# The way out of a convolution branch by seven products of quarters, with its weights' sums and the mixing's sums made by transfers in DRAM

## The chip, the cores and the metric

The kernel runs on one core of one Trainium2 chip. A core has five engines with an instruction queue each: TensorE (PE, matrix products; PEld is its weight load), VectorE (DVE), ScalarE (ACT), GpSimd (POOL) and SyncE (SP, which starts most transfers). Sixteen DMA engines move data between DRAM and the on-chip buffers, or from DRAM to DRAM. The metric is the device time of one execution in microseconds.

## The reference

One block of a decoder over 512 tokens of width 1024, all in float32. The part that matters here lies between two token mixers and the residual:

```python
z_glu, z_rx, z_rg, z_ga, z_gb = jnp.split(h @ w_in[l] + b_in[l], split_idx, axis=-1)

u = z_glu[..., :D_CONV] * jax.nn.sigmoid(z_glu[..., D_CONV:])
u = causal_depthwise_conv(u, conv_dw_w[l], conv_dw_b[l])
u = jax.nn.silu(layernorm(u, conv_ln_g[l], conv_ln_b[l]))
y_a = u @ conv_w_out[l] + conv_b_out[l]                    # 512x1024 by 1024x1024
...
y_b = (hb * jax.nn.gelu(z_rg, approximate=True)) @ lru_w_out[l]   # 512x1280 by 1280x1024

m = jax.nn.sigmoid(z_ga) * y_a + jax.nn.sigmoid(z_gb) * y_b
x = x + m @ w_mix_out[l]                                   # 512x1024 by 1024x1024

h = rmsnorm(x, norm2_g[l])
x = x + (jax.nn.silu(h @ ffn_w1[l]) * (h @ ffn_w3[l])) @ ffn_w2[l]
```

## The kernel before

**Products.** Every float32 operand is split into a high part (a cast to fp32r on ACT, `split_to`, L127) and a low part (full minus high, by `sub`, L123, on DVE or POOL), and a product is three matmuls: high by high, high by low, low by high. Channels lie along the 128 partitions and the 512 tokens along the columns, until the mixing turns to tokens by partition.

**Stages.** z is the way in, with the depthwise convolutions, the gates and the recurrence run beside it; yb the recurrence's way out (8 tiles of 128 channels); ya the convolution branch's way out (8 tiles); mxr the mixing's product; fr (L1443) and or the channel mixer. The layer norm of the convolution branch (`conv_norm`) runs beside z and yb: lnms is the all-reduce over partitions of the column sums, lnvs that of the squares, both on POOL; after lnvs ACT takes the root (lnvp) and DVE its RECIPROCAL, and then the eight tiles u are scaled, passed through Silu and split into un.

**ya.** Tile j takes one 1024x128 chunk of `conv_w_out` (co, `w_tiles`), 24 matmuls of 512 columns into one PSUM bank (`mm3`), then on DVE one operation that adds the bias and multiplies by the gate sga, and two adds of 256 columns with yb into mxu and mxv, the mixing's inputs. `mixq.order()` sets the order of the tiles to 0, 4, 1, 5, ..., so that pairs for the mixing come early.

**The mixing and the channel mixer** already use seven products. `Quartered` describes a weight matrix in quarters b11, b12, b21, b22 and its sums t1 = b12 + b11, t3 = b22 + b12, t2 = t3 + b11, t4 = t2 + b21. `Sevenfold` makes the sums of the inputs (`pair`) and runs the seven products in two halves (`run`): the first opens banks r1, r2 and r5, and adds the first two into the residual x (the operations x<-mxr on DVE); the second half opens r1 again and reuses the other banks. For the mixing, `make_sums` loads rows of w_mix_out (mxws) and makes the sums on DVE, four adds for each of four row pairs: t1 and t4 stay on chip and are split there, t2 and t3 are stored to DRAM (mxt) and loaded later as chunks. For the channel mixer's second matrix, `dram_sums` makes the sums (ot) in DRAM by eight transfers for each slice, started by POOL: a copy t <- b (L487), an adding transfer t <- t + b (L488); a step that needs an earlier one waits for its landing.

**Weights** come in chunks in a fixed order (`wchunk`): SP loads a chunk into one of 8 raw buffers (raw), ACT casts it into one of 5 hl buffers, DVE or POOL takes the low part; `weights` emits chunks AHEAD = 4 beyond the one in use. LO_BY_DVE = 6 says that the chunks lo0 to lo5 of yb are split by DVE, lo6 and lo7 by POOL.

**Order.** On PE, ACT, DVE and SP the instructions run in the order of the program, in which work beside a stage is dealt out by generators (`run_beside`); on POOL a scheduler sets the order ahead of time. Each engine works through its queue in order: what waits holds up all behind it.

Of the kernel before, what the change touches and what calls it, by code (L numbers as in the profile page):

```python
# [13 lines left out]
P = 128  # L14
# [43 lines left out]
SUMS_OWN = 40  # L58
LO_BY_DVE = 6


MIX_LATE_LAG, LATE_LAG = 2, 8

# [22 lines left out]
def tile_block(ctx, tc, a, out):  # L86
# [38 lines left out]
    def split_to(h, l, full, eng, copy=act.copy):  # L125

        copy(h, full)  # L127
# [145 lines left out]
    IN_PLACE = ("t2", "t1", "t4", "t3")  # L273

    class Quartered:
        def __init__(self, name, w, kh, lo, parts=(), step=None, on_pool=(), put_off=()):
# [11 lines left out]
            def quarter(n, k):  # L288
                if n[0] == "t":
                    assert self is mixq or out_made  # L290
# [40 lines left out]

        def make_sums(self, k):
            q = [raws.tile([P, 1024], F32, tag="raw", name=f"{self.name}ws{k}_{i}") for i in range(2)]
            for i, v in enumerate(q):
                nc.sync.dma_start(v, self.w[:, self.tile(k, i), :])
            (q11, q12), (q21, q22) = ((v[:, :T], v[:, T:]) for v in q)
            add(q22, q22, q12)
            add(q12, q12, q11)
            add(q11, q22, q11)
            add(q21, q21, q11)  # L340
            for n, v in (("t1", q12), ("t2", q11), ("t3", q22), ("t4", q21)):
                if n in self.parts:
                    self.parts[n][k] = split(f"{self.name}{n}{k}", v, vec)
                else:
                    nc.sync.dma_start(self.sums[n, k], v)
# [137 lines left out]
    def dram_sums(quarter, sums):  # L483
# [5 lines left out]
        return [(copy, t1, b11), (plus, t1, b12), (copy, t3, b12), (plus, t3, b22), (copy, t2, t3), (plus, t2, b11), (copy, t4, t2), (plus, t4, b21)]  # L489

    def out_sums():

        rows = outq.w.rearrange("p (k i) n -> p i k n", i=2)
        jobs = []
        for k0 in range(0, KF, OUT_SUMS_OF):
            ks = slice(k0, min(k0 + OUT_SUMS_OF, KF))
            jobs.append(dram_sums(lambda i, h: rows[:, i, ks, h * T : (h + 1) * T], {n: v[:, ks, :] for n, v in outq.all_sums.items()}))
# [3 lines left out]
        out_made.append(True)  # L501

    for k in BEGUN:
        for n in ("b11", "b21"):
            f_both(n, k, pool_e if (n, k) == ("b11", 2) else None if k == BEGUN[0] else vec)

# [351 lines left out]

    u, un, lanes, held_back = [], [], [], []
    ended, total = [], []  # L860
# [27 lines left out]
    def column_sums(name, tot):  # L888
# [3 lines left out]
        return sums  # L892

    def conv_norm():
        mean = bank2("lnmp")
        sums = column_sums("lnms", total[0])
        yield True
        for _ in range(MEAN_LAG):
            yield True
        act.activation(mean, sums, AF.Copy, scale=1.0 / DC)  # L900
        yield True
        tot = longt("lnvt")
        for c in range(8):
            sub(vec, u[c], u[c], mean)
            q = tot if c == 0 else shortt(f"sq{c}")
            act.activation(q, u[c], AF.Square)
            yield True
            if c:
                vec.tensor_tensor(out=tot, in0=tot, in1=q, op=ALU.add)
# [7 lines left out]
        vec.reciprocal(rs, rs)  # L917
        for _ in range(6):
            yield True
        for c in range(8):  # L920
# [3 lines left out]
            un.append(split(f"un{c}", u[c], vec))  # L924
            yield True

    lanes += [conv_lane(0), conv_lane(1)]
# [192 lines left out]

    sgb, sga = [None] * 8, [None] * 8

    def sig(base, j, ps, dest, name):
        dest[j] = longt(f"{name}{j}")
        act.activation(dest[j], ps, AF.Sigmoid, bias=b_in(base + j))
        yield 0

    def half_sig(j, ps):
        sgb[j] = longt(f"sgb{j}")
        act.activation(sgb[j], ps, AF.Tanh, scale=0.5, bias=b_in(GB + j))  # L1130
        yield 0
# [20 lines left out]
    f_sums_steps = make_f_sums()  # L1152
    out_made = []
    out_steps = out_sums()
    with tc.manual_schedule(engines={ET.PE, ET.Activation, ET.DVE, ET.SP}):
        for kind, j in ORDER:
            next(f_sums_steps, None)
            if kind == "u" and j < EARLY:
                for _ in glu(j, in_mm(GLU + j), in_mm(GLU + 8 + j)):
# [14 lines left out]
            elif kind == "ga":  # L1174
                later(sig(GA, j, step(GA, j), sga, "sga"), 1)
            elif kind == "h":
# [17 lines left out]
    yb = sgb  # L1194
    run_beside(1000)


    LO, HI = HALVES

    class Sevenfold:
        def __init__(self, q, lag=0, behind=False):
            self.lag, self.kept, self.behind = lag, 0, behind
            self.q, self.uv, self.ops, self.waiting = q, [], [], []  # L1210
            self.name, self.kh = q.name, q.kh
# [17 lines left out]
        def pair(self, k, ua, va):  # L1229
# [10 lines left out]
            add(e[:, LO], ua[:, HI], va[:, LO])  # L1240
            self.ops.append((u_, sp, e, va))

# [7 lines left out]
        def run(self, sums, begun, end):  # L1250
# [10 lines left out]
            def split_late():  # L1261
                k = len(late)
                if k < kh:
                    late.append((split(f"{n}eb{k}", self.ops[k][2], vec), split(f"{n}vb{k}", self.ops[k][3], vec)))

            r1, r2 = ([bank(f"{n}{r}{i}") for i in range(2)] for r in ("r1", "r2"))
# [25 lines left out]
            def third(i, ks, closing=kh - 1, cs=slice(0, T), banks=None, opening=None):  # L1292
                for k in ks:
                    self.product(banks or r1, i, quarter(late[k][1], HI), *get(k, "t4"), k == opening, k == closing, not banks, cs)

            for k in range(kh - 1):
                second(k, *get(k, "b22", "t2", "t3"))
                split_late()
# [7 lines left out]
            act.activation(warm, late[-1][1][0][:, :1].bitcast(F32), AF.Sqrt, scale=0.0, bias=eps_t)  # L1306
            last = get(kh - 1, "b22", "t2", "t3", ahead=AHEAD - 1)
            end(lambda: second(kh - 1, *last), plus, less, r1, r2, r7, third)

    m7 = Sevenfold(mixq, MIX_LATE_LAG, True)  # L1310
    for n, j in enumerate(mixq.order()):
        ws = w_tiles(f"co{j}", ND)
        ps = bank(f"ya{j}")
        mm3(ps, ws, un)
        o = sga[j]
        vec.scalar_tensor_tensor(out=o, in0=ps, scalar=pc("conv_b_out", j), in1=o, op0=ALU.add, op1=ALU.mult)
        m7.tile(j, lambda cs, dst: add(dst, o[:, cs], yb[j][:, cs]))
        if n == 0:
            mixq.make_sums(3)
        if n == 5:  # L1320
            x2 = [[longt(f"x2{t}{h}") for h in range(2)] for t in range(NT)]
            for t in range(NT):
                for h in range(2):
                    nc.sync.dma_start(x2[t][h], x_nat[:, t, h * T : (h + 1) * T])
        next(f_sums_steps, None)

# [65 lines left out]

    m7.run(x2, lambda k: None, mix_end)


# [342 lines left out]
```

## Time and profile before

| | |
|---|---|
| time, median of 3 runs | 786.16 us (785.57 to 787.25) |
| the profiled execution | 785.74 us, span 784.0 us |
| granted TensorE clock | 0.999 |
| busy: PE, DVE, ACT, POOL | 99%, 85%, 60%, 33% of the span |
| DMA | 158.65 MB, 202 GB/s in the mean |

The profile is of one execution. Busy times don't add up to the span, since engines run side by side. In lists of instructions, the first number is the start in microseconds from the span's beginning, the second the duration; a group xN is N instructions in a row. Names are written out <- in, and L is the line of the kernel.

### The profile page before, as it was taken

To read this page: it belongs to the slowest core of one execution; us is meant where nothing else is said; L and a number is where in the kernel's file an instruction comes from. 1 tells how busy PE (TensorE), PEld (TensorE's weight loads), DVE (VectorE), ACT (ScalarE), POOL (GpSimd) and SP (SyncE) were. 2 spreads that over 40 slices of the span, in tenths; PEclk is the share of its full clock that TensorE was granted. 3 is DMA by queue.
4 is the path that set the end of the run, shared out by engine and by line. 5 is a ranking of instruction groups with operands and counts; after the bars stand their busy time and mean duration, and the time that the engine had idled before them with its cause. 6 is when DMAs were issued, how large, how long until landed. Compare 5 with 4: busy or idle time off the path is not lost.

```text
span 784.0 us, 12205 instructions
## 1 busy us (share of the span) xinstructions
PE 776.4 (99%) x4325; PEld 679.2 (87%) x4325; DVE 667.9 (85%) x1007; ACT 473.8 (60%) x696; POOL 262.5 (33%) x209
## 2 busy tenths in 40 slices
PE   8999999999999999999999999999999999999997
PEld 8988888888888888888888898999999999888886
DVE  6489998899887996999767869779888889999957
ACT  8543678976785687575234676555554555666844
POOL 3366856577555753130000461312212220000001
PEclk9999999999999999999999999999999999999999
DMA  8827978796783555378565466997989794679522
GB/s 246 233 58 212 250 216 229 201 247 188 210 247 120 165 156 164 120 241 251 199 198 160 153 229 216 233 307 192 270 240 246 250 213 126 230 236 297 171 67 108
DMA packets 181199, 158.65 MB, mean 202 GB/s; under 512 B 14202, under 2 KB 146450, under 8 KB 181138
## 3 DMA queue, kind: packets, MB, share of 16 engines
q1 hardware_dynamic: 171186, 132.43, 57.7%
q0 software_dynamic: 9792, 25.17, 13.1%
q8 instruction: 34, 0.56, 0.3%
q10 hardware_dynamic: 160, 0.27, 0.1%
q14 instruction: 27, 0.22, 0.1%
HBM read 132.14 MB, written 35.65 MB: 214 GB/s over the span
## 4 chain that ended last, share of the span: by engine, by line
PE 98%; DMA 1%; DVE 0%; ACT 0%; SPq 0%; issue 0%
PE z L622 36%; PE fr L1443 25%; PE or L1248 13%; PE yb L622 7%; PE ya L622 6%; PE mxr L1248 5%; PE f L622 3%; PE g L1074 2%; PE fr L1506 1%; DMA x<-in_x_dram 1%; PE tx L683 0%; PE th L667 0%; PE z L740 0%; ACT of L1680 0%; PE orl L1248 0%; DVE n1j L704 0%
## 5 line engine op out<-in xcount | busy, mean ns | idle before, releaser
L875 DVE SCALAR_TENSOR_TENSOR cv<-u,par,cv 128x507 f32<-128x507 f32 (+15 forms) x240 | 162.1, 732 | 4.0 <-ACT cv L871 3.3
L123 POOL TENSOR_TENSOR hl_in<-raw_in,hl_in 128x1024 fp32r<-128x1024 f32 (+1 forms) x52 | 122.8, 2373 | 87.4 <-ACT hl_in L127 83.3
L1443 PE MATMUL fr<-hs_0h,hl_ft 128*128 128x256 f32 x320 | 59.2, 283 | 0.0
L127 ACT CAST hl_in<-raw_in 128x1024 fp32r<-128x1024 f32 x50 | 51.4, 1047 | 1.6 <-PE z L622 0.8
L1443 PEld LDWEIGHTS fr<-hs_0h,hl_ft 128*128 128x128 f32 x320 | 50.6, 192 | 0.0
L1443 PE MATMUL fr<-hs_0l,hl_ft 128*128 128x256 f32 x160 | 45.3, 283 | 0.0
L127 ACT CAST hl_fb<-raw_fb 128x1024 fp32r<-128x1024 f32 x30 | 31.3, 1046 | 23.1 <-PE fr L1443 10.9
L488 POOL DMA_DIRECT2D ot<-in_ffn_w_dram x24 | 26.4, 1112 | 54.2 <-DVE hl_ft L123 32.7
L123 DVE TENSOR_TENSOR hl_fb<-raw_fb,hl_fb 128x1024 fp32r<-128x1024 f32 x29 | 35.3, 1221 | 10.4 <-ACT hl_fb L127 10.4
L123 POOL TENSOR_TENSOR hl_ot<-raw_ot,hl_ot 128x1024 fp32r<-128x1024 f32 x1 | 2.4, 2410 | 121.3 <-ACT hl_ot L127 121.3
L622 PE MATMUL z<-h10h,hl_in 128*128 128x512 f32 (+1 forms) x108 | 41.1, 382 | 0.0
L622 PE MATMUL z<-h12h,hl_in 128*128 128x512 f32 (+1 forms) x108 | 40.8, 379 | 0.0
L622 PE MATMUL z<-h13h,hl_in 128*128 128x512 f32 (+1 forms) x108 | 40.8, 379 | 0.0
L622 PE MATMUL z<-h14h,hl_in 128*128 128x512 f32 (+1 forms) x108 | 40.8, 379 | 0.0
L622 PE MATMUL z<-h15h,hl_in 128*128 128x512 f32 (+1 forms) x108 | 40.8, 379 | 0.0
L622 PE MATMUL z<-h16h,hl_in 128*128 128x512 f32 (+1 forms) x108 | 40.8, 379 | 0.0
L622 PE MATMUL z<-h11h,hl_in 128*128 128x512 f32 (+1 forms) x108 | 40.8, 379 | 0.0
L622 PE MATMUL z<-h17h,hl_in 128*128 128x512 f32 (+1 forms) x108 | 40.8, 379 | 0.0
L127 ACT CAST hl_ft<-raw_fb 128x1024 fp32r<-128x1024 f32 x28 | 28.6, 1048 | 15.0 <-DVE raw_fb L114 11.8
L127 ACT CAST hl_ob<-raw_ob 128x1024 fp32r<-128x1024 f32 (+1 forms) x23 | 23.3, 1015 | 21.1 <-PE or L1248 14.7
L115 POOL TENSOR_TENSOR fws<-fws 128x256 f32<-128x256 f32 x44 | 34.1, 774 | 2.4
L123 DVE TENSOR_TENSOR hl_ft<-raw_fb,hl_ft 128x1024 fp32r<-128x1024 f32 x28 | 33.6, 1218 | 1.2 <-ACT hl_ft L127 1.2
(948 smaller groups left out, 2589.9 us busy)
## 6 DMA issues: line engine op xcount, KB each, us to landing
raw_in<-in_w_in_dram SPq DMA_DIRECT2D x51, 512.0 KB
raw_fb<-in_ffn_w_dram SPq DMA_DIRECT2D x74, 256.0 KB
ot<-in_ffn_w_dram POOLq DMA_DIRECT2D x30, 512.0 KB, 8.6
raw_ob<-in_ffn_w_dram SPq DMA_DIRECT2D x33, 256.0 KB
raw_ot<-ot SPq DMA_DIRECT2D x33, 256.0 KB
fws<-in_ffn_w_dram SPq DMA_DIRECT2D x12, 512.0 KB
raw_lo<-in_lru_w_out_dram SPq DMA_DIRECT2D x16, 320.0 KB
ot<-ot POOLq DMA_DIRECT2D x10, 512.0 KB, 6.2
```

Of the source, the lines that this page charges most:

```text
L115: plus_on = lambda eng, o, x, y: eng.tensor_tensor(out=o, in0=x, in1=y, op=ALU.add)
L123: return eng.tensor_tensor(out=o, in0=x, in1=y, op=ALU.subtract)
L127: copy(h, full)
L488: plus = lambda o, x: pool_e.dma_start(o, x, accum_op=ALU.add)
L622: pe.matmul(ps, l, r, start=i == 0, stop=i == n - 1)
L875: vec.scalar_tensor_tensor(out=acc[:, s:], in0=u[c][:, : T - s], scalar=dw(c, s), in1=acc[:, s:], op0=ALU.mult, op1=ALU.add)
L1074: pe.matmul(ps[:HB], head_chunk[0][:ROWS_G, g, h % 2, m, :], ext[h][m][:ROWS_G], start=m == 0, stop=m == 1)
L1248: pe.matmul(banks[i][:, cs], l_[:, ts], r_[:, cs], start=start and n == 0, stop=stop and n == 2, skip_group_check=again)
L1443: pe.matmul(ps[:, HALVES[i]], lw[:, c, :], rx_, start=not (again or i or c or m), stop=bool(i and c == 3 and m == 2), skip_group_check=True,)
L1506: pe.matmul(self.r4[:, HALVES[i]], lw, rx_, start=not (i or c or m), stop=bool(i and c == 3 and m == 2), skip_group_check=True)
```

## The change

1. The convolution branch's way out is made of quarters. For two groups g of output columns (`CO_PAIRS`), seven products of 128-channel blocks with 256 tokens each: r1 = a11·b11, r2 = a12·b21, r3 = s4·b22, r1 += s2·t2, r5 = s1·t1, r7 = s3·t3, r1 += a22·t4. The inputs' sums s1 to s4 are made on DVE (`ya_sums`) and split (`ya_sum_parts`); gates and results are kept by halves of the tokens (`by_tokens`), so that yb's tiles become the mixing's inputs in place. The weights come as 14 chunks (cob11, cob21, cob22, cot2, cot1, cot3, cot4 for two groups) instead of 8.
2. The sums of the weights of this product and of the mixing are made by `dram_sums`, 16 transfers of 512 KB each (`mid_sums`), started by POOL; `make_sums` goes. The mixing's t1 and t4 are loaded as chunks too.
3. LO_BY_DVE becomes 8, MIX_LATE_LAG 1, the mixing fetches its chunks one less ahead in places, and some splits of the channel mixer's first chunks change between DVE and POOL.

The core of the diff:

```diff
-LO_BY_DVE = 6
+LO_BY_DVE = 8
+MID_AT, MID_STEP = 60, 4
-MIX_LATE_LAG, LATE_LAG = 2, 8
+MIX_LATE_LAG, LATE_LAG = 1, 8
...
-    for j in [0, 4, 1, 5, 2, 6, 3, 7]:
-        wchunk(f"co{j}", conv_out[:, :, j * P : (j + 1) * P], ND, P, lo=vec)
+    CO_PAIRS = ((0, 1), (3, 2))
+    co_sums = {n: dram.tile([P, 2, 4, 2 * P], F32, tag=f"co{n}", name=f"co{n}") for n in IN_PLACE}
...
+    CO_ORDER = [(n, g) for of in (("b11", "b21"), ("b22", "t2", "t1", "t3", "t4")) for g in range(2) for n in of]
...
-    mixq = Quartered("mx", a["w_mix_out"][0].rearrange("(k p) n -> p k n", p=P), ND // 2, vec, ("t1", "t4"), put_off=("b22_2",))
+    mixq = Quartered("mx", a["w_mix_out"][0].rearrange("(k p) n -> p k n", p=P), ND // 2, vec, step=2, on_pool=("t4_0",), put_off=("b22_2",))
...
+    def mid_sums():
+        co_jobs = [dram_sums(lambda i, h: co_quarter(f"b{i + 1}{h + 1}", g), {n: v[:, g] for n, v in co_sums.items()}) for g in range(2)]
+        for name, of in (("co", co_jobs), ("mx", sums_jobs(mixq, 2))):
+            for start, dst, src in (one for step in zip(*of) for one in step):
+                with tc.issue_after(newest["sub"]):
+                    start(dst, src)
+                yield
+            sums_made.append(name)
...
+    def ya_sums(k):
+
+        a1, a2 = u[k], u[k + 4]
+        sub(vec, a2[:, HI], a1[:, HI], a2[:, HI])
+        sub(vec, a1[:, HI], a1[:, LO], a1[:, HI])
+        sub(vec, a1[:, LO], a2[:, HI], a1[:, LO])
+        add(a2[:, LO], a2[:, LO], a1[:, LO])
...
+            if n >= MID_AT:
+                next(mid_steps, None)
...
-        vec.scalar_tensor_tensor(out=sgb[j], in0=sgb[j], scalar=1.0, in1=ps, op0=ALU.add, op1=ALU.mult)
+        for o, cs in by_tokens(j, sgb, "sgb"):
+            vec.scalar_tensor_tensor(out=o, in0=o, scalar=1.0, in1=ps[:, cs], op0=ALU.add, op1=ALU.mult)
         run_beside(7)
         next(f_sums_steps, None)
-        if j in (2, 4, 6):
-            mixq.make_sums(j // 2 - 1)
+        for _ in range(MID_STEP):
+            next(mid_steps, None)
...
-    for n, j in enumerate(mixq.order()):
-        ws = w_tiles(f"co{j}", ND)
-        ps = bank(f"ya{j}")
-        mm3(ps, ws, un)
-        o = sga[j]
-        vec.scalar_tensor_tensor(out=o, in0=ps, scalar=pc("conv_b_out", j), in1=o, op0=ALU.add, op1=ALU.mult)
-        m7.tile(j, lambda cs, dst: add(dst, o[:, cs], yb[j][:, cs]))
...
+    def ya_group(g):
+        k1, k2 = CO_PAIRS[g]
+
+        def product(ps, x_, w_, again=False):
+            h, l = weights(f"co{w_}_{g}")
+            for i in range(2):
+                cols = slice(i * P, i * P + P)
+                for c, (xh, xl) in enumerate(ya_in[x_]):
+                    for m, (lw, rx_) in enumerate(((h, xh), (h, xl), (l, xh))):
+                        pe.matmul(
+                            ps[:, HALVES[i]], lw[:, c, cols], rx_, start=not (again or i or c or m),
+                            stop=bool(i and c == 3 and m == 2), skip_group_check=True,
+                        )
+            return ps
...
+        r1 = product(bank(f"ya1_{g}"), "a11", "b11")
+        c11 = biased("c11", r1, k1)
+        r2 = product(bank(f"ya2_{g}"), "a12", "b21")
+        add(c11, r2, c11)
+        mixed(c11, k1, 0)
+        yield
+        r3 = product(bank(f"ya3_{g}"), "s4", "b22")
+        product(r1, "s2", "t2", True)
+        q = biased("q", r1, k2, -1.0)
+        r5 = product(bank2(f"ya5_{g}"), "s1", "t1")
+        add(q, r5, q)
+        c12 = shortt(f"c12_{g}")
+        add(c12, r3, q)
+        mixed(c12, k2, 0)
+        r7 = product(bank(f"ya7_{g}"), "s3", "t3")
+        sub(vec, q, q, r7)
+        mixed(q, k2, 1)
+        made(k2)
+        c21 = biased("c21", r7, k1)
+        product(r1, "a22", "t4", True)
+        add(c21, r1, c21)
+        mixed(c21, k1, 1)
+        made(k1)
+        yield
```

`biased` is an Identity on ACT with scale and bias, two of 256 columns; `mixed` multiplies by the gate and adds yb's half, on DVE; `made` hands a pair to the mixing.

How the change orders two engines, in rows of the program (name, shape, and a count where rows are alike). On POOL, around the two all-reduces, before (fs is a sum for the channel mixer, hl_lo a low part of yb's weights):

```order
L443 DMA fs3_82<-fws3_1_1_3031 128x4x256
L891 ISA
L891 ISA lnms_3024<-lnmt_1069 128x512
L891 ISA lnvs_3268<-lnvt_3148 128x512
L123 ISA
L123 TENSOR_TENSOR hl_lo6_0_3335<-raw_lo6_0_3333,hl_lo6_0_3335 128x640
L123 TENSOR_TENSOR hl_lo6_1_3340<-raw_lo6_1_3338,hl_lo6_1_3340 128x640
```

And in the changed kernel (L493 is the copying and L494 the adding transfer of `dram_sums`, L911 the all-reduce):

```order
L911 ISA lnms_3044<-lnmt_1077 128x512
L494 DMA cot1_79<-in_conv_w_out_dram 128x4x256 x2
L493 DMA cot3_81<-in_conv_w_out_dram 128x4x256 x2
L493 DMA mxt1_83<-in_w_mix_out_dram 128x2x512
L494 DMA cot3_81<-in_conv_w_out_dram 128x4x256 x2
L493 DMA mxt1_83<-in_w_mix_out_dram 128x2x512
L493 DMA cot2_78<-cot3_81 128x1024 x2
L494 DMA mxt1_83<-in_w_mix_out_dram 128x2x512
L494 DMA cot2_78<-in_conv_w_out_dram 128x4x256
L911 ISA lnvs_3301<-lnvt_3171 128x512
L494 DMA cot2_78<-in_conv_w_out_dram 128x4x256
L493 DMA cot4_80<-cot2_78 128x1024
```

Twelve transfers have come between lnms and lnvs, and the four splits of lo6 and lo7 have left the queue. On DVE, in ya, what stands around a tile before:

```order
L1316 SCALAR_TENSOR_TENSOR sga4_2972<-ya4_3643,par_95,sga4_2972 128x512
L114 TENSOR_TENSOR mxu0_3616<-sga4_2972,sgb4_2065 128x256
L114 TENSOR_TENSOR mxv0_3617<-sga4_2972,sgb4_2065 128x256
L123 TENSOR_TENSOR hl_co3_3686<-raw_co3_3684,hl_co3_3686 128x1024
L123 TENSOR_TENSOR mxus0l_3672<-mxu0_3616,mxus0h_3671 128x512
L123 TENSOR_TENSOR mxs10_3675<-mxv0_3617 128x256
L123 TENSOR_TENSOR mxe0_3680<-mxu0_3616,mxv0_3617 128x256
L123 TENSOR_TENSOR mxs1p0_3677<-mxs10_3675,mxs1p0_3677 128x256
L123 TENSOR_TENSOR mxv0_3617<-mxs10_3675,mxu0_3616 128x256
L114 TENSOR_TENSOR mxe0_3680<-mxu0_3616,mxv0_3617 128x256
L1316 SCALAR_TENSOR_TENSOR sga1_2684<-ya1_3689,par_95,sga1_2684 128x512
```

And around the seventh and eighth products (r5 and r7 of the first group) of the changed kernel:

```order
L124 TENSOR_TENSOR hl_cot2_1_3834<-raw_cot2_1_3832,hl_cot2_1_3834 128x1024
L115 TENSOR_TENSOR q_0_3828<-ya5_0_3831,q_0_3828 128x512
L115 TENSOR_TENSOR c12_0_3862<-ya3_0_3769,q_0_3828 128x512
L124 TENSOR_TENSOR hl_cot1_1_3869<-raw_cot1_1_3867,hl_cot1_1_3869 128x1024
L1394 TENSOR_TENSOR c12_0_3862<-c12_0_3862,sga1_0_2796 128x512
L124 TENSOR_TENSOR q_0_3828<-q_0_3828,ya7_0_3866 128x512
L115 TENSOR_TENSOR sgb1_0_1371<-c12_0_3862,sgb1_0_1371 128x512
L1394 TENSOR_TENSOR q_0_3828<-q_0_3828,sga1_1_2797 128x512
L124 TENSOR_TENSOR hl_cot3_1_3917<-raw_cot3_1_3915,hl_cot3_1_3917 128x1024
L115 TENSOR_TENSOR sgb1_1_1372<-q_0_3828,sgb1_1_1372 128x512
L124 TENSOR_TENSOR mxus1l_3900<-sgb1_0_1371,mxus1h_3899 128x512
L124 TENSOR_TENSOR mxs11_3903<-sgb1_1_1372 128x256
```

In place of one operation on the product and two adds for each tile, DVE has one operation out of PSUM, two on halves of tokens, and a split of a chunk, for each product, with the pairs for the mixing between them.

More of the change, by code (lines that the diff above doesn't have):

```diff
@@ L125, in split_to @@
     def split_to(h, l, full, eng, copy=act.copy):
-        copy(h, full)
+        newest["cast"] = copy(h, full)
         if eng is None:
@@ L919, in conv_norm @@
             yield True
-        for c in range(8):
+        for c in [0, 4, 1, 5, 2, 6, 3, 7]:
             vec.tensor_tensor(out=u[c], in0=u[c], in1=rs, op=ALU.mult)
@@ L1293, in third @@
                 for k in ks:
-                    self.product(banks or r1, i, quarter(late[k][1], HI), *get(k, "t4"), k == opening, k == closing, not banks, cs)
+                    self.product(banks or r1, i, quarter(late[k][1], HI), *get(k, "t4", ahead=self.ahead), k == opening, k == closing, not banks, cs)
             for k in range(kh - 1):
-                second(k, *get(k, "b22", "t2", "t3"))
+                with tc.issue_after(newest["late"]) if self.behind and k == kh - 2 else nullcontext():
+                    got = get(k, "b22", "t2", "t3", ahead=self.ahead if k == kh - 2 else AHEAD)
+                second(k, *got)
                 split_late()
@@ L1306, in run @@
             act.activation(warm, late[-1][1][0][:, :1].bitcast(F32), AF.Sqrt, scale=0.0, bias=eps_t)
[L1307 removed]
+            with tc.issue_after(newest["late"]) if self.behind else nullcontext():
+                last = get(kh - 1, "b22", "t2", "t3", ahead=AHEAD - 1)
             end(lambda: second(kh - 1, *last), plus, less, r1, r2, r7, third)
[L1310 to L1325 removed]
+    m7 = Sevenfold(mixq, MIX_LATE_LAG, True, AHEAD - 1)
@@ L1327, in tile_block @@
+    groups = [ya_group(g) for g in range(2)]
+    for g in groups:
+        next(g)
+    ya_sum_parts()
+    next(groups[0])
+    x2 = [[longt(f"x2{t}{h}") for h in range(2)] for t in range(NT)]
+    for t in range(NT):
+        for h in range(2):
+            nc.sync.dma_start(x2[t][h], x_nat[:, t, h * T : (h + 1) * T])
+    next(groups[1])
     for _ in f_sums_steps:
@@ L1393, in tile_block @@
     m7.run(x2, lambda k: None, mix_end)
+    assert not put_off
     o7 = Sevenfold(outq, LATE_LAG)
```

120 lines of the change are left out of this document (82 added, 38 removed).

## The prediction

> **What bounds the kernel now.** I began with the page's busy times and the chain that ended last, then read the chain in order of time.
>
> ```profile
> span 784.0 us, 12205 instructions
> PE 776.4 (99%) x4325; PEld 679.2 (87%) x4325; DVE 667.9 (85%) x1007; ACT 473.8 (60%) x696; POOL 262.5 (33%) x209
> ...
> PE 98%; DMA 1%; DVE 0%; ACT 0%; SPq 0%; issue 0%
> ```
> ```profile
> 310.61 54.40 PE yb L622 x240
> 365.01 43.52 PE ya L622 x192
> 408.53 35.36 PE mxr L1248 x156
> ...
> 497.81 175.68 PE fr L1443 x1464
> ```
>
> TensorE is the bound: 98% of the chain is its own work. From yb through ya to mxr each piece starts where the last one ended, so in the stages of the change every microsecond of PE is a microsecond of the kernel, and every new wait of PE as well. The profiled execution took 785.74 us, 1.74 more than its span, and 0.42 less than the median of 786.16; I sum against 785.74 and add the 0.42 at the end.
>
> **The products (TensorE).** Before, ya is 192 matmuls of 512 columns: 43.52/192 = 226.7 ns each. Afterwards it is 2 groups x 7 products x 24 = 336 matmuls of 256 columns. Before has that width in the channel mixer: 175.68/1464 = 120.0 ns each. That is more than half of 226.7 (113.3), and this row shows why.
>
> ```profile
> core 0: us, PE busy (x) PEld busy (x) DVE busy (x) ACT busy (x) POOL busy (x), PEclk, DMA share, GB/s
> ...
> 575.00:600.00 25.00, 25.00 (x210) 25.00 (x210) 22.11 (x26) 14.22 (x19) 7.32 (x8) 1.00 0.98 213
> ```
>
> In those 25 us weight loading (PEld) is never idle: 210 loads, 119 ns each, set the pace. So ya becomes 336 x 0.1200 = 40.32 us, and the gain is 43.52 - 40.32 = **3.20 us**, not the eighth (5.44) that the count of products promises. The ends are 0.1133 (38.1 us, gain 5.4) and 0.1200; I take 0.1200, since the new matmuls also have a weight load each. [...]
>
> **The sums' transfers (GpSimd's queue).** 32 transfers of 512 KB, each copying or adding in DRAM, are put between lnms and the end of the branch. GpSimd works in order, and lnvs, the all-reduce of the variance, now stands behind 14 of them, 12 of which come after lnms. What it waits for is a chain: copy t3, add to t3 (waits for that copy), copy t2 from t3 (waits for that add), and the issue of the add to t2, which waits for that copy.
>
> ```profile
> 304.92 3.75 POOL L891 PARTITION_ALL_REDUCE lnms<-lnmt  x1 [5.70 <-DVE y9l L123]
> 325.72 3.65 POOL L891 PARTITION_ALL_REDUCE lnvs<-lnvt  x1 [17.05 <-DVE lnvt L909]
> ```
> ```profile
> L488 POOL DMA_DIRECT2D ot<-in_ffn_w_dram x24: 843/1135/1467, 492.5 to 640.9; - x24
> ...
> DMA to landing us min/median/max: 6.0/9.0/12.0
> ```
> ```profile
> L487 POOL DMA_DIRECT2D ot<-ot x12: 515/522/559, 560.3 to 620.7; - x12
> ...
> DMA to landing us min/median/max: 3.3/6.4/7.4
> ```
> ```profile
> q1 hardware_dynamic: 171186, 132.43, 57.7%
> q0 software_dynamic: 9792, 25.17, 13.1%
> ```
> ```profile
> 300.00:315.00 15.00, 15.00 (x68) 12.40 (x67) 9.05 (x13) 10.57 (x16) 3.75 (x1) 1.00 0.58 185
> 315.00:330.00 15.00, 15.00 (x68) 12.43 (x67) 14.72 (x21) 7.50 (x12) 3.65 (x1) 1.00 0.42 121
> ```
>
> L488 is an adding transfer, L487 a copying one. lnms ends at 308.67; two adds are issued (2 x 0.84), so the copy of t3 goes out at 310.4. With medians: 310.4 + 6.4 + 9.0 + 6.4 + 1.14 (issue) = 333.3, and lnvs ends 3.65 later, at **T = 337.0**, against 329.37 before. The ends: shortest landings give 310.4 + 3.3 + 6.0 + 3.3 + 0.84 = 323.8, earlier than lnvt is ready (325.72), so T stays 329.4; longest give 310.4 + 7.4 + 12.0 + 7.4 + 1.47 + 3.65 = 342.3. I take the medians, which come from stretches with the DMA engines 98% busy, because these will be as busy: q0's 13.1% of 784 us is 103 us for some 48 such transfers, 2.1 us of all sixteen engines each; 14 of them before lnvs are 29 us in some 39, on top of the 0.42 to 0.58 there. [...]
>
> **What waits behind lnvs, on DVE.**
>
> ```profile
> 330.29 3.36 DVE L917 RECIPROCAL lnvp<-lnvp 128x512 f32<-128x512 f32 x1
> 333.56 0.81 DVE L123 TENSOR_TENSOR hl_lo<-raw_lo,hl_lo 128x640 fp32r<-128x640 f32 x1
> ```
> ```profile
> 390.01 0.42 DVE L123 TENSOR_TENSOR mxs<-mxv 128x256 f32<-128x256 f32 x1
> 390.35 0.42 DVE L123 TENSOR_TENSOR mxe<-mxu,mxv 128x256 f32<-128x256 f32 x1
> ...
> 391.25 0.42 DVE L123 TENSOR_TENSOR mxv<-mxs,mxu 128x256 f32<-128x256 f32 x1
> 391.70 0.42 DVE L114 TENSOR_TENSOR mxe<-mxu,mxv 128x256 f32<-128x256 f32 x1
> ...
> 421.49 2.73 DVE L114 TENSOR_TENSOR x<-mxr,x 128x512 f32<-128x512 f32 x4 [3.77 <-PE mxr L1248]
> 424.14 0.68 DVE L123 TENSOR_TENSOR mxeb1l<-mxe,mxeb1h 128x512 fp32r<-128x512 f32 x1
> 424.74 1.22 DVE L123 TENSOR_TENSOR hl_mxt<-raw_mxt,hl_mxt 128x1024 fp32r<-128x1024 f32 x1
> 425.88 0.68 DVE L123 TENSOR_TENSOR mxvb1l<-mxv,mxvb1h 128x512 fp32r<-128x512 f32 x1
> ```
> ```profile
> L1316 DVE SCALAR_TENSOR_TENSOR sga<-ya,par,sga 128x512 f32<-128x512 f32 x8 | 6.0, 750 | 9.9 <-PE ya L622 9.5
> ```
>
> Start to start, DVE's operations cost 0.34 us (256 columns), 0.45 where one needs its forerunner (391.25 to 391.70), 0.60 (512), 0.66 (512 out of PSUM, 2.65/4), 1.14 (1024), 3.27 (the reciprocal); 0.74 for 640 is taken between 0.60 and 1.14. Counted in the new order, from the reciprocal to the first add of the mixer's product into x stand 1 reciprocal, 12 + 40 of 256, 6 of 640, 43 + 10 of 512 and 23 of 1024: 3.3 + 17.7 + 4.4 + 25.8 + 6.6 + 26.2 = 84.0. Before it was 1, 36, 3, 57 and 15, or 69.1 (all 512 at 0.60), and the idle time in ya (9.9) and ahead of the add (3.77) was its cover. Sixteen adds for the mixer's sums go (9.6), but splits of 14 chunks in place of 8, sums of the inputs, mixing by token halves and four splits that GpSimd did (LO_BY_DVE) come.
>
> PE wants that add done when it opens r1's bank again in the mixer's second half.
>
> ```profile
> 426.05 0.62 PE L1248 MATMUL mxr<-hl_mxt,mxvb0h 128*128 128x512 f32 x2
> ...
> 427.41 0.62 PE L1248 MATMUL mxr<-hl_mxb,mxeb0h 128*128 128x512 f32 x2
> ```
>
> Without new waits that moment is 426.05 - 3.20 = 422.85. The add ends at T + 0.92 (329.37 to 330.29) + 84.0 + 0.68 + some 1.5 for operations on a forerunner's result = T + 87.1. The second add follows 1.26 later while PE wants it 0.68 later, another 0.58. So PE stalls S = T + 87.1 - 422.85 + 0.58 = T - 335.2, which is 1.8 at T = 337.0.
>
> There is a **floor that T doesn't move**. DVE can't split cot2_1 before its cast, and ACT does that after q, which needs the sixth product: 365.01 + 6 x 24 x 0.120 = 382.3, then two activations of 0.41 and a cast of 1.05.
>
> ```profile
> 386.85 1.05 ACT L127 CAST hl_mxb<-raw_mxb 128x1024 fp32r<-128x1024 f32 x1 [4.39 <-PE ya L622]
> ...
> 390.46 0.41 ACT L127 CAST mxs1p<-mxs 128x256 fp32r<-128x256 f32 x1 [1.79 <-DVE mxs L123]
> ```
>
> So at 384.2 DVE begins 13 of 1024, 20 of 256, 19 of 512 and 8 out of PSUM: 38.3 us, the add itself 0.68, some 0.7 for forerunners: 423.9, or a stall of 1.0 + 0.58 = **1.6**. The floor's ends are 0 (DVE waits nowhere and PE's demand is read too early) and 3 (each wait for a cast or product costs another 0.1 to 0.2). I take S = 1.6 to 1.8, so 1.7. Afterwards nothing gives it back: PE has no idle time to shrink.
>
> **What else moves, and lies beside.** SP's queue meets the residual's x loads earlier, ahead of half of mxt2_1, whose place in the raw buffers waits for DVE's split of mxb21_0 (near 399 by the prices above), so they go out at about the same time as before, and are needed at that same add, 20 us later.
>
> ```profile
> 401.38 4.07 SPq L1324 DMA_DIRECT2D x<-in_x_dram  x8
> ```
>
> The loads of weights: minus 8 of 512 KB and 8 stores of 256, plus 8 of 256 and 6 of 512, about even at q1's 0.577 x 784/132.43 = 3.4 us per MB. The transfers' 68 us nearly fill the engines from 298 to 400. Followed link by link from T with 6.4 a copy and 9.0 an add, the branch's last sum (t4) lands near 361 and the mixer's near 400; the loads that wait for them on SP, with the channel mixer's first weights behind, get their raw buffers only some 10 us after that. GpSimd's freed time (four splits) and the two new splits for the channel mixer fall where it is idle. If that cover fails, PE waits for a weight, rival 3.
>
> **The sum.** 785.74 - 3.20 + 1.7 = 784.2, and 0.4 more against the median: **784.6**, 1.6 us or 0.2% below; 0.2% (1.57 us) is also about what a measurement of this kernel can tell from no change.
>
> **Rivals.**
> 1. The queue is no matter: transfers land in 3.3 and 6.0 us, T stays below 336, and the floor is at its low end, 0 to 1. For it: 0.42 DMA share at 315 to 330, and 3.77 us of slack ahead of the add. Against: 69 us of DVE's work became 84. Time 783.0 to 783.9.
> 2. The other side: lnvs behind the queue decides. Back-to-back adds and copies queue behind each other, and T passes 340.0, where S = 4.8 and the kernel is 0.2% slower; that takes three landings of 24.8 us together instead of 21.8. The longest rows give T = 342.3, S = 7.1, 790.0. For it: six adds and six copies are issued within some 25 us, and landings of 12.0 are seen. Against: the stretch was half empty.
> 3. The DMA engines are over-full and a chunk of weights or a sum comes late. 68 us of transfers on 0.42 to 0.80 busy stretches leave no room between 300 and 409. If each of some 12 links down to the mixer's t4 takes 1.5 us more, it lands 18 us late, past that 10, and holds back SP's queue and the first weights of the channel mixer: 3 to 8 us, 786 to 791. Against: in 575 to 600 the engines are 98% busy and PE is idle nowhere.
> 4. The narrow matmul costs 0.113: 5.4 instead of 3.2 gained; but PE then comes to the same add 2.2 earlier and waits there, 784.8 by T, or 783.6 where the floor alone rules (its sixth product ends 1.0 earlier, so the stall grows by 1.2).
>
> **Chances.** Forecast (S 1 to 4) 0.45, of which 0.22 faster and 0.23 same. Rival 1: 0.18, faster. Rival 2: 0.20, slower. Rival 3: 0.12, 0.05 same and 0.07 slower. Rival 4: 0.05, 0.02 faster and 0.03 same. Together faster 0.42, same 0.31, slower 0.27. The range leaves out the low tail below 782.8 and rival 2 above 788.6.
>
> **What would show it.** The chain's ya pieces with 0.120 us per matmul (40.3 in all). lnvs starting near 333 with a wait for a DMA, not for lnvt. DVE idle ahead of lnvp's reciprocal, then full until near 425. A wait of PE for x<-mxr at the second half of mxr, 1 to 3 us; no wait of PE in yb. I am wrong if PE waits inside ya for a chunk or a sum (rival 3), if yb's last tiles wait, or if no wait of PE shows at all.

## The result, and the profile after

The changed kernel takes **797.66 us** (median, 796.81 to 799.2) where the one before takes 785.94 on the same chip: a ratio of 1.0148, 95% interval 1.0126 to 1.0171, so 11.7 us or 1.5% slower. I had forecast 784.6 within 782.8 to 788.6.

The page of the changed kernel, busy times, GpSimd's DMA queue and the shares of the chain:

```profile
span 796.7 us, 12616 instructions
PE 778.4 (98%) x4469; PEld 684.9 (86%) x4469; DVE 673.6 (85%) x1028; ACT 490.0 (62%) x734; POOL 294.0 (37%) x240
...
q0 software_dynamic: 18496, 41.95, 22.5%
...
PE 85%; DMA 6%; DVE 3%; issue 2%; POOL 2%; ACT 1%; POOLq 0%; DVEq 0%; SPq 0%; ACTq 0%
```

The chain was TensorE's for 98% before and is for 85% now: other engines have come into the path. Where, the chain in order of time says (start, duration, what):

```profile
313.97 2.38 POOL cot L494 x2
316.35 14.74 DMA cot<-in_conv_w_out_dram
331.38 11.59 DMA cot<-in_conv_w_out_dram
...
347.19 3.23 POOL lnvs L911
...
378.14 17.29 PE ya L1381 x144
...
461.03 10.06 PE fr L1555 x84
```

From 314 to 350 the path is GpSimd's queue: a copying transfer of t3 that lands after 14.74 us, an adding one after 11.59, then lnvs, which ends at 350.4. The chain leaves PE a second time from 395.47 to 437.18, for DVE and then for loads of x (11.68 us from 419.39) and of a chunk of the mixing's sums, but PE waits only 0.8 us at the end of that stretch. PE's own list of waits, and its instructions around them:

```profile
PE yb L642 <- ACT hl_lo L128: 5.7, 1, 5.7
PE yb L642 <- DVE hl_lo L124: 2.9, 1, 2.9
...
PE mxr L1304 <- DVE x L115: 0.8, 1, 0.8
```
```profile
311.92 0.39 PE L642 MATMUL yb<-y0h,hl_lo 128*128 128x512 f32 x1
...
351.82 0.80 PE L642 MATMUL yb<-y0h,hl_lo 128*128 128x512 f32 x1 [5.74 <-ACT hl_lo L128]
...
356.55 0.63 PE L642 MATMUL yb<-y1h,hl_lo 128*128 128x512 f32 x1
356.97 0.63 PE L642 MATMUL yb<-y1l,hl_lo 128*128 128x512 f32 x1
```

The wait of yb is not for lnvs itself. ACT's root (lnvp) stands in ACT's queue ahead of two casts of yb's weights, and DVE's reciprocal ahead of their splits:

```profile
350.44 0.69 ACT L967 ACTIVATE lnvp<-lnvs,eps_t 128x512 f32<-128x512 f32 x1 [19.28 <-POOL lnvs L911]
351.06 1.34 ACT L128 CAST hl_lo<-raw_lo 128x640 fp32r<-128x640 f32 x2
```

Both engines sat still, ACT for 19.28 us, with work behind them that PE needed. After the waits the matmuls come 0.42 us apart (356.55, 356.97) instead of 0.227, and the table by stretches gives the granted clock and the DMA share (the two columns ahead of the last; the share adds up packet times and can pass 1):

```profile
330.00:338.00 8.00, 8.00 (x37) 6.60 (x37) 0.71 (x1) 1.15 (x1) 2.11 (x3) 1.00 1.16 266
...
346.00:354.00 8.00, 1.31 (x3) 0.50 (x2) 2.84 (x1) 3.25 (x4) 5.55 (x3) 0.74 1.03 153
354.00:362.00 8.00, 6.04 (x18) 4.85 (x19) 8.00 (x16) 4.73 (x9) 3.17 (x5) 0.61 1.01 244
```

The two spans differ by 12.7 us, and stage by stage: yb starts 1.3 later (311.92 against 310.61; that lag is from the start of the kernel and varies between runs); it takes 378.14 - 311.92 = 66.2 instead of 54.4, that is 11.8 more, of which 8.65 are the two waits and 3.2 the slower clock; ya, at 17.29/144 = 120.1 ns a matmul, takes 40.3 instead of 43.5, 3.2 less; and from its end (418.5) to the channel mixer's fr (461.03) it takes 42.6, where before it was 448.41 - 408.53 = 39.9, 2.7 more. 1.3 + 11.8 - 3.2 + 2.7 = 12.6.

```profile
448.41 10.07 PE fr L1443 x84
```

### The profile page after: what moved, and what is told of

Same layout as the page of the kernel before. It is cut to its first block, busy times and chain, and to the rows that moved or that the text cites. A ratio compares the mean times of both kernels' runs of the same rounds, so it can differ in the third digit from the quotient of the medians.

```text
span 796.7 us, 12616 instructions
## 1 busy us (share of the span) xinstructions
PE 778.4 (98%) x4469; PEld 684.9 (86%) x4469; DVE 673.6 (85%) x1028; ACT 490.0 (62%) x734; POOL 294.0 (37%) x240
## 3 DMA queue, kind: packets, MB, share of 16 engines
q0 software_dynamic: 18496, 41.95, 22.5%
## 4 chain that ended last, share of the span: by engine, by line
PE 85%; DMA 6%; DVE 3%; issue 2%; POOL 2%; ACT 1%; POOLq 0%; DVEq 0%; SPq 0%; ACTq 0%
PE z L642 35%; PE fr L1555 24%; PE or L1304 13%; DMA cot<-in_conv_w_out_dram 3%; PE yb L642 3%; PE f L642 3%; PE ya L1381 2%; PE g L1128 2%; PE mxr L1304 2%; DMA x<-in_x_dram 1%; DMA raw_mxt<-mxt 1%; PE fr L1618 1%; DVE hl_cot L124 1%; DVE xs L1457 0%; POOL cot L494 0%
## 5 line engine op out<-in xcount | busy, mean ns | idle before, releaser
L494 POOL DMA_DIRECT2D ot<-in_ffn_w_dram x24 | 26.4, 1112 | 54.4 <-DVE hl_ft L124 31.6
L124 DVE TENSOR_TENSOR hl_fb<-raw_fb,hl_fb 128x1024 fp32r<-128x1024 f32 x27 | 33.2, 1229 | 10.3 <-ACT hl_fb L128 9.8
L128 ACT CAST hl_ft<-raw_fb 128x1024 fp32r<-128x1024 f32 x28 | 28.6, 1049 | 15.2 <-DVE raw_fb L115 11.8
## 6 DMA issues: line engine op xcount, KB each, us to landing
mxt<-in_w_mix_out_dram POOLq DMA_DIRECT2D x12, 512.0 KB, 10.1
```

The source lines that it names most:

```text
L124: return eng.tensor_tensor(out=o, in0=x, in1=y, op=ALU.subtract)
L128: newest["cast"] = copy(h, full)
L494: plus = lambda o, x: pool_e.dma_start(o, x, accum_op=ALU.add)
```

## The experiments

My theory after the result: 14 transfers ahead of lnvs make it late, and that is the loss. The rivals: the transfers' load on the DMA engines is the loss wherever lnvs stands; and something else of the change (DVE's added work, GpSimd's splits).

### Nothing but the products: no_transfers

```diff
     if n[0] == "t":
-        return co_sums[n][:, g]
+        n = {"t1": "b11", "t2": "b12", "t3": "b21", "t4": "b22"}[n]
 ...
     for start, dst, src in (one for step in zip(*of) for one in step):
-        with tc.issue_after(newest["sub"]):
-            start(dst, src)
         yield
```

> The changed kernel without any of the 32 transfers: the loads of the sums read quarters of the weights instead, so the products are of other numbers, while their count, shape and order stay. It times the seven products and DVE's work alone. Theory: the transfers cost all that was lost; 3.2 us of gain less up to 2 us of stall at the mixer: 783 to 785.5. Rival (DVE's added work bounds): PE waits 3 us or more at the mixer's second half, 786 to 788.

Measured: 786.93 us (786.58 to 788.08) beside 785.66, ratio 1.0018 (1.0009 to 1.0028), above the 783 to 785.5 of my theory. So the 32 transfers cost 10.7 us in all, and without them the change is still not faster. The chain shows the products' gain in full, and where it went:

```profile
364.92 40.31 PE ya L1380 x336
...
439.77 4.71 PE mxr L1303 x12
...
449.37 10.06 PE fr L1554 x84
```

ya is 3.2 shorter, but from the mixer's start (405.23) to fr it is 44.1 us instead of 39.9. One wait of 1.9 (for DVE's stats) stands ahead of the 12 matmuls at 439.77, and these take 4.71 instead of 12 x 0.227 = 2.7. DVE was late there because GpSimd now makes low parts at the same time. Here GpSimd first, then DVE, and last the like DVE rows of before:

```profile
429.66 3.10 POOL L124 TENSOR_TENSOR hl_mxt<-raw_mxt,hl_mxt 128x1024 fp32r<-128x1024 f32 x1 [99.86 <-DMA raw_fb<-in_ffn_w_dram]
```
```profile
430.42 2.89 DVE L124 TENSOR_TENSOR mxvb3l<-sgb,mxvb3h 128x512 fp32r<-128x512 f32 x1
...
442.51 3.40 DVE L1456 TENSOR_SCALAR xs<-x,stats 128x512 f32<-128x512 f32 x3
```
```profile
433.30 0.69 DVE L123 TENSOR_TENSOR mxvb3l<-mxv,mxvb3h 128x512 fp32r<-128x512 f32 x1 [0.27 <-ACT mxvb3h L127]
...
442.70 1.28 DVE L1346 TENSOR_SCALAR xs<-x,stats 128x512 f32<-128x512 f32 x3
```

Beside GpSimd's split the same operation takes 2.89 us and not 0.69, ending as the split ends (433.3 after 432.8), and beside a later one (443.25 to 445.63) three of xs take 3.40 and not 1.28. What holds DVE while the split runs, these rows don't show.

### GpSimd's splits: no_transfers_dve_lows

```diff
-    mixq = Quartered(..., step=2, on_pool=("t4_0",), put_off=("b22_2",))
+    mixq = Quartered(..., step=2, put_off=("b22_2",))
 ...
-        f_both(n, k, vec if (n, k) == ("b21", 2) else pool_e)
+        f_both(n, k, pool_e if (n, k) == ("b11", 2) else vec)
```

> As no_transfers (786.93 us), and besides the low parts of mxt4_0, fb11_1 and fb21_1 are taken by DVE instead of GpSimd. Theory (GpSimd's splits at the mixer's end hold up DVE, whose operations took 2.89, 2.08 and 3.40 us there instead of 0.60, 1.14 and 1.28; PE waited 1.9 and then ran 12 matmuls in 4.7 us instead of 2.7): wait and slow matmuls go, 783 to 784.5. Rival (DVE is simply full there: 44.3 busy of 45 us, and 3 more splits of 1.14 come to it): the wait grows, 787 to 790.

Measured: 784.93 us (784.74 to 786.15) beside 785.64, ratio 0.9991 (0.9982 to 1.0), hardly told from no change, and 2.0 us less than no_transfers. Its xs group takes 1.28 again, and fr starts at 447.67. So GpSimd's splits cost 2.0 us, and the products alone, without the price of any sum, are worth 0.7 us of the 3.2: from the mixer's start (405.34) to fr the kernel still takes 42.3 us instead of 39.9. Two waits of PE for DVE at the mixer's end (1.1 for stats, 0.5 for x) are 1.6 of these 2.4; the rest is spread over the pieces behind them, at a mean granted clock of 0.999 in the profiled execution.

### lnvs ahead of the queue: lnvs_first

```diff
-MID_AT, MID_STEP = 60, 4
+MID_AT, MID_STEP, MID_BEFORE = 60, 8, 6
 ...
+    while len(begun_mid) >= MID_BEFORE and "norm" not in newest:
+        yield
-    with tc.issue_after(newest["sub"]):
+    with tc.issue_after(newest["norm"] if len(begun_mid) >= MID_BEFORE else newest["sub"]):
         start(dst, src)
```

> The changed kernel, with six of the 32 transfers before lnvs and all others queued behind it, so that lnvs waits for no landing. Theory (lnvs stands behind transfers that wait for each other): lnvs starts near 329 to 331 instead of 346.7, PE waits nowhere in yb (8.65 us of waits gone) and the 3.0 us of half-speed matmuls after them go too: some 11.7 us less than the changed kernel, 785 to 787. Rival (the DMA engines are over-full, and weights come late wherever the queue stands): the sums now start some 4 us later, PE waits in ya or mxr for a cot or mxt chunk, 788 to 793. Rival (DVE's added work): PE waits 3 us or more at the mixer's second half, 787 to 789.

Measured: **802.09 us** (801.58 to 804.88), ratio 1.0207 (1.019 to 1.0224). My theory missed by 15 us. What stands behind lnvs is dealt out eight transfers a step instead of four. lnvs does start at 328.50 and yb has no wait, but the loss comes back later, and larger:

```profile
328.50 1.36 POOL lnvs L914
...
332.41 10.15 DMA cot<-in_conv_w_out_dram
...
360.57 11.72 DMA cot<-cot
...
379.57 11.44 DMA raw_cot<-cot
```
```profile
PE mxr L1309 <- ACT mxeb1h L128: 8.8, 1, 8.8
```

The chain t3, t2, t4 and the load of t4 take 59 us one after the other. The mixing's sums come later still, and PE's longest wait falls there. ACT's rows show why it is for mxeb1h: this cast stands behind that of a chunk of the mixing's sums, which ACT waits 12.03 us for.

```profile
434.09 1.04 ACT L128 CAST hl_mxt<-raw_mxt 128x1024 fp32r<-128x1024 f32 x1 [12.03 <-DMA raw_mxt<-mxt]
...
435.56 0.61 ACT L128 CAST mxeb1h<-mxe 128x512 fp32r<-128x512 f32 x1
```

So removing the wait for lnvs doesn't remove the loss: a second limit lay just behind it.

### The load without the lateness: lnvs_first_unread

As lnvs_first, with the loads of the sums reading the quarters in place (the first diff of no_transfers).

> As lnvs_first (802.09 us), with the same 32 transfers in the same places, but nothing reads the sums: the loads of cot and mxt read quarters of the weights (other numbers). What is left of the transfers is their load on the DMA engines. Theory (DMA engines over-full; loads of weights slow down whoever reads them): 793 or more, with PE's waits in ya and mxr. Rival (the sums come late, since each link waits for the one before, and the loads stand behind them on SP's queue): most of the loss over no_transfers goes, 787 to 790.

Measured: 795.56 us (795.42 to 796.85), ratio 1.0129 (1.0115 to 1.0143). Nothing waits for a sum or for lnvs here; the transfers only fill the DMA engines (share 1.09 from 365 to 405 us, 0.53 in no_transfers). It is still 8.6 us over no_transfers, and lnvs_first 6.5 over it. The chain:

```profile
416.36 8.68 DMA raw_mxt<-in_w_mix_out_dram
...
426.49 10.53 DMA raw_mxt<-in_w_mix_out_dram
```

Loads of the mixer's chunks, on SP's queue, now end the waits. So the load is a limit of its own, worth 8.6 us when PE comes on time, and the late sums another 6.5 on top. That is the load with 26 of the 32 transfers behind lnvs, a later place than in the changed kernel.

### What makes the transfers slow: copies_only

```diff
+    def copies_of(q, sums):
+        return [(pool_e.dma_start, o, x) for _, o, x in dram_sums(q, sums)]
```

used for all 32 transfers in place of `dram_sums`.

> The changed kernel with each of the 16 adding transfers turned into a plain copy of the same size and place (the sums are then other numbers). Theory (the adding transfers, some 10 to 15 us each here, make the chain before lnvs long and fill the DMA engines): the chain of copy, copy, copy lands some 8 to 12 us earlier, lnvs starts at 334 to 339 instead of 346.7, PE waits 0 to 2 us in yb, 787 to 791. Rival (a transfer within DRAM costs the same whether it adds or not): within 2 us of the changed kernel, 795.5 to 799.5.

Measured: **787.09 us** (786.79 to 787.45), ratio 1.0018 (1.0009 to 1.0027): 10.6 us less than the changed kernel, with the same count of transfers, the same bytes, the same chain of waits, and 0.2 over no transfers at all. lnvs ends at 341.2:

```profile
337.96 3.19 POOL L914 PARTITION_ALL_REDUCE lnvs<-lnvt  x1
```

The list of DMA issues, first of the changed kernel, then of this one (last column: median us to landing), and this one's q0 row:

```profile
cot<-in_conv_w_out_dram POOLq DMA_DIRECT2D x12, 512.0 KB, 10.9
```
```profile
cot<-in_conv_w_out_dram POOLq DMA_DIRECT2D x12, 512.0 KB, 6.8
```
```profile
q0 software_dynamic: 14400, 41.95, 19.5%
```

Packet time follows from the q0 rows: 13.1% of 784.0 before is 102.7 us of all sixteen engines, 19.5% of 785.5 is 153.2, and 22.5% of 796.7 is 179.3. So 32 copies cost 50.5 us, 1.58 each; turning 16 of them into adding ones costs 26.1 more, or 3.2 for each adding transfer: twice a copy, with 4096 more packets for the same bytes.

### The transfers added to the kernel before: before_plus_transfers

```diff
-LO_BY_DVE = 6
+LO_BY_DVE = 8
+    co_spare, mx_spare = ...   # sums in DRAM that nothing reads
+    def mid_sums():            # the same 32 transfers, dealt at the same places of yb
```

> The kernel before, with 32 such transfers in the same places on GpSimd's queue, which nothing reads, and lo6 and lo7 split by DVE (otherwise they would stand behind the transfers too). Nothing of the seven products is in it. Theory (the queue before lnvs): lnvs ends near 348 to 350, PE waits 6 to 9 us in yb and then runs at a lower granted clock, 9 to 13 us more than before: 795 to 799. Rival (over-full DMA engines): waits in ya and mxr for weights, none in yb, 788 to 795. Rival (DVE's added work): no wait of PE, 786 to 787.

Measured: 805.33 us (803.42 to 805.7), ratio 1.0245 (1.023 to 1.026), a loss of 19.7 without any of the change's products, above the 795 to 799 expected and 8 us more than the change itself loses. lnvs starts at 342.01, and the two waits in yb are those of the changed kernel. The 3.2 for un7l is of another kind: this kernel still makes the mixing's sums on DVE, and the split un7l stands there behind an add for them (mxws, 381.86) that waited 5.82 us for a transfer. So load comes in here beside lateness, and the run doesn't part the two:

```profile
PE yb L643 <- ACT hl_lo L127: 6.1, 1, 6.1
PE ya L643 <- DVE un7l L123: 3.2, 1, 3.2
PE yb L643 <- DVE hl_lo L123: 2.2, 1, 2.2
```

### The lateness without the load: late_lnvs_1, late_lnvs_3, late_lnvs_6

no_transfers, and ahead of lnvs one row of its input goes through DRAM and back, TRIP copies on the way:

```diff
+    pool_e.dma_start(trip[0], tot[:1, :])
+    for i in range(TRIP):
+        pool_e.dma_start(trip[i + 1], trip[i])
+    pool_e.dma_start(tot[:1, :], trip[TRIP])
     sums = column_sums("lnvs", tot)
```

> This is no_transfers (the loads of sums read quarters, no sums are made) with one thing added: before lnvs, a row of its input goes to DRAM, is copied there once, and comes back, three transfers of 2 KB in a chain. [...] Theory (lateness of lnvs reaches PE only when the last weights of yb wait behind the reciprocal on DVE, which the runs so far put at an end of lnvs of about 340): no wait in yb, time 786.5 to 788. Rival (DVE's queue behind the reciprocal is full, so that every us of lateness is a us of PE, as S = T - 335.2 of the prediction says): a wait of 2 us or more in the mixer's second half on top of the 1.9 of no_transfers, time 788.5 to 790.

> As late_lnvs_1 with three copies in the chain, five transfers of 2 KB, lnvs ending near 342. Theory: a wait of 1 to 3 us in yb for hl_lo, and the slower clock behind it, time 788.5 to 791.5. Rival (only the DMA load of the big transfers hurts, the lateness is taken up by DVE's idle time in ya): 786.5 to 787.5.

> As late_lnvs_1 with six copies in the chain, eight transfers of 2 KB, lnvs ending near 350, as in the changed kernel, with a DMA share in yb as low as before. Theory (the whole loss of the changed kernel is the lateness of lnvs): waits of 8 to 9 us in yb for hl_lo, about 3 us of slower clock, and the time of the changed kernel, 796.5 to 798.5. Rival (the load of the transfers itself takes a part): 791 to 795.5, the rest of the changed kernel's 797.7 being the load.

Measured: 790.23 (ratio 1.0064, 1.0047 to 1.008), 796.14 (1.0136, 1.0121 to 1.0151) and 803.54 (1.0231, 1.0216 to 1.0246), beside 785.49. The ends of lnvs that I expected rested on a guess for the time of a link, which no run shows. A link took 3.2 to 3.3 us in the mean (the three of late_lnvs_1 from 326.67 to 336.40, the eight of late_lnvs_6 from 326.64 to 353.30), so lnvs ended later; the root on ACT starts at its end:

```profile
339.67 0.69 ACT L972 ACTIVATE lnvp<-lnvs,eps_t 128x512 f32<-128x512 f32 x1 [3.26 <-POOL lnvs L911]
```
```profile
346.44 0.69 ACT L972 ACTIVATE lnvp<-lnvs,eps_t 128x512 f32<-128x512 f32 x1 [6.67 <-POOL lnvs L911]
```
```profile
356.57 0.69 ACT L972 ACTIVATE lnvp<-lnvs,eps_t 128x512 f32<-128x512 f32 x1 [6.63 <-POOL lnvs L911]
```

All three expectations missed in their numbers. Read by the end of lnvs, the last two give 7.4 us for 10.1 of lateness, and at 350.4, the end in the changed kernel, 796.1 + 4.0 x 0.73 = 799.0: a lateness of that size without load costs as much as the whole loss, 797.7. That is no proof that the same waits are at work. One caution: with the chain, the root and the reciprocal also stand some rows later in their queues (in late_lnvs_6 all casts of hl_lo come ahead of the root), so the waits fall in ya, for un and ys, and not in yb. That order is a difference of its own: late_lnvs_1 (339.7) is 3.1 us over copies_only (341.2), though lnvs ends earlier.

### The sums elsewhere: sums_early and co_early_mix_before

```diff
-MID_AT, MID_STEP = 60, 4
+MID_AT, MID_STEP = 24, 4
```

> The changed kernel with the 32 transfers dealt out over the last 36 steps of z (from about 150 us) instead of over yb, so that the last has landed before lnms. Theory (the queue before lnvs): PE's waits in yb are gone, and so is the over-full DMA from 322 to 440; 3.2 us of gain less what is lost at the mixer's end: 783 to 786. Rival (the DMA engines are full in z as well): weights of z come late, PE waits in z for hl_in, 788 or more. Rival (DVE's added work): no wait in yb but 2 to 3 us at the mixer's second half, 785 to 787.

Measured: 798.3 us (794.77 to 801.57), ratio 1.016 (1.0122 to 1.0198). lnvs waits for nothing but its input, but z is now late, as the first rival had it: PE waits there for low parts that GpSimd makes between transfers, loads of weights for z stand in the chain (one of 8.26 us at 186.72), and yb starts at 318.52 instead of 310.61. The wait, and a row of the chain:

```profile
PE z L642 <- POOL hl_in L124: 5.4, 3, 3.2
```
```profile
318.52 54.40 PE yb L642 x240
```

The other version sends only the 16 transfers of the convolution branch early, at every second step, and makes the mixing's sums on DVE as before:

```diff
-LO_BY_DVE = 8
-MID_AT, MID_STEP = 60, 4
+LO_BY_DVE = 6
+MID_AT, MID_STEP = 22, 4
 ...
+        if j in (2, 4, 6):
+            mixq.make_sums(j // 2 - 1)
```

> The seven products with 16 transfers only, for conv_out's sums, one in every second step of z from about 130 us; the mixing's sums by loads and adds on DVE as in the kernel before, lo6, lo7 and the channel mixer's first splits on the engines of before. Theory (what is gained is 3.2 us, what is lost comes from the transfers' place and load and from GpSimd's splits at the end): 783.5 to 787, if z takes 16 transfers without waits. Rival (z's DMA engines can't take them): PE waits in z, 788 to 793. Rival (DVE's added work): PE waits 3 us or more in ya or mxr, 787 to 790.

Measured: 788.53 us (788.07 to 789.1), ratio 1.0037 (1.0024 to 1.0049). z and yb have no waits; PE waits 4.1 us in ya for DVE, whose work is now the larger, as the second rival had it. Two of the three waits:

```profile
PE ya L1398 <- DVE ys_1l L124: 2.1, 1, 2.1
...
PE ya L1398 <- DVE un7l L124: 1.1, 1, 1.1
```

It is 9.1 us better than the changed kernel and 2.9 worse than the one before. Since even sums for nothing leave only 0.7 (no_transfers_dve_lows), I found no version that beats the kernel before.

## Why the prediction was wrong

- **The products**: right. 120.0 ns a matmul and 40.32 us were forecast; 120.1 and 40.3 were measured, and no_transfers has 40.31.
- **The end of lnvs, T = 337.0**: this step failed first. It was 350.4, past even my longest case of 342.3, and rival 2's mechanism decided. Along the chain: lnms ended 5.3 later than before (313.97; 1.3 of it is the run's late start, and the rest comes with the transfers in the program: lnms starts at 309.30 in copies_only, behind a low part on DVE, and at 305.07 in no_transfers), the two adds took 2.38 to issue instead of 1.68, and copy, add, copy and issue took 347.19 - 316.35 = 30.8 instead of 22.9; lnvs itself was 0.4 shorter. The mis-sized terms are the landings: 14.74 and 11.59 where I took 6.4 and 9.0. I took medians from a stretch with 98% busy engines as what a busy stretch does, but there 48 transfers were spread over some 187 us (issued from 453.6 to 640.9); here five were issued within 5 us of each other (rows below), and adding ones take twice the packet time (3.2 us against 1.58, copies_only). I had averaged the two kinds to 2.1 us each, so 68 us in all where the runs have 76.6.

GpSimd's rows in the changed kernel:

```profile
313.85 2.78 POOL L494 DMA_DIRECT2D cot<-in_conv_w_out_dram  x2
315.57 2.60 POOL L493 DMA_DIRECT2D cot<-in_conv_w_out_dram  x2
317.09 1.77 POOL L493 DMA_DIRECT2D mxt<-in_w_mix_out_dram  x1
```

- **What waits behind lnvs**: I followed DVE's queue and priced the wait at the mixer's second half, S = T - 335.2. Missing was the other queue behind lnvs: ACT's root holds two casts of yb's weights. Waits of 5.7 and 2.9 in yb came, which I had only named as a sign of being wrong. With the measured T = 350.4 the formula gives S = 15.2 and 798.1 us, 0.4 from the result; that is luck, for the wait that it prices, the one for x, was 0.8. DVE's count was near: from the end of lnvs to the end of the add into x I had 87.1 us, and 86.7 passed. What fell is the moment at which PE wants that add. I held it at 422.85, and PE, late by its waits in yb, came at 436.4, so the two delays overlap and are not added. In copies_only it is the same on a smaller scale: T = 341.2, where S would be 6.0 and the time about 788.5, and it took 787.09 with 1.8 of wait in yb and 0.8 for x. There the loss in yb is in part given back later: from the mixer's start to fr it takes 42.6 us instead of the 44.1 of no_transfers. The 9.2 us of lateness from 341.2 to 350.4, and the load of the adding transfers with them, then cost 10.6.
- **The floor of 1.6 that T doesn't move**: it wasn't there. In no_transfers lnvs ends at 329.8, the add ends at 422.5 where I had 423.9, and PE doesn't wait for it (first row; the second is the changed kernel's add):

```profile
421.86 0.68 DVE L115 TENSOR_TENSOR x<-mxr,x 128x512 f32<-128x512 f32 x1
```
```profile
436.44 0.68 DVE L115 TENSOR_TENSOR x<-mxr,x 128x512 f32<-128x512 f32 x1
```

- **The DMA engines' load**: "the transfers' 68 us nearly fill the engines" was written down, and then given only 0.12. lnvs_first and lnvs_first_unread show that this rival alone gives 8.6 to 15.2 us. In the changed kernel it is mostly covered: PE comes late by lnvs, and the sums and chunks then come in time (PE waits nowhere in ya, and 0.8 us in the mixer's second half). The two limits are not added; the removal of one uncovers the other.
- **GpSimd's splits "fall where it is idle"**: GpSimd was idle, DVE was not, and it was held: 2.0 us, by no_transfers_dve_lows.
- **The price of a wait**: I counted a microsecond of PE's wait as one. In yb the clock added 3.2 to 8.65. In the profiled execution of no_transfers it added 2.0 to a wait of 1.9, but hardly to the kernel's time: of its ten executions the four with a mean granted clock of 0.999 took 787.0 us in the mean, and the six at 0.996 to 0.998 took 787.2.

## What to carry to other kernels

When transfers or other work are put into an in-order queue ahead of a reduction, list for every engine what stands behind the reduction's consumers, ACT's casts as well as DVE's splits. Price the transfers by engine time over the stretch that they must fit in, adding ones at double (3.2 us against 1.58 here), and take landing times from a stretch that is as crowded as the new one will be. Before changing the place of what looks late, leave it out altogether: here that one run showed that the gain to be had was too small for any place.

## What the runs showed of the hardware

- **An adding transfer from DRAM to DRAM** of 512 KB took 3.2 us of packet time on all sixteen DMA engines, a copying one 1.58, for the same bytes (q0 of the changed kernel and of copies_only).
- **The granted clock fell after one short wait and not after others.** Soon after a wait of 1.86 us in no_transfers, matmuls of 512 columns came up to 0.5 us apart for about 3 us, and the mean clock of these 6 us is 0.72:

```profile
438.00:444.00 6.00, 4.24 (x11) 3.06 (x12) 5.72 (x14) 2.98 (x7) 0.75 (x1) 0.72 0.85 251
```

In the changed kernel, behind waits of 5.74 and 2.91 us, they came 0.42 us apart, and the mean clock from 350 to 360 us was 0.50. Behind a wait of 1.78 us in copies_only the mean clock from 340 to 365 us was 1.00, behind one of 1.51 us in sums_early the matmuls came 0.23 us apart, and the profiled execution of co_early_mix_before, with one of 2.1 us, had a mean clock of 0.999, like that of the kernel before. What sets the moment wasn't tried.
- **A small transfer from DRAM to DRAM** of 2 KB, chained to the one before on GpSimd's queue, took 3.45 us from issue to issue in late_lnvs_6, with a DMA share of 0.51 from 330 to 350 us (links at 329.61 and 350.32, six steps apart).
